# Attention with a bias: q and k land as whole rows, and each head is transposed in its own half of the array's columns

## The chip, the cores and the metric

The kernel runs on one core of one Trainium2 chip. The metric is the device time of one execution in microseconds. Before the change the median of three runs is 240.04 us (239.69 to 240.31).

TensorE (PE) multiplies matrices: a weight load (PEld) puts a tile of 128 rows into the array, a matmul streams the other operand past it and writes to PSUM. ScalarE (ACT) and VectorE (DVE) read PSUM and SBUF, GpSimd (POOL) and SyncE (SP) issue the DMAs here.

## The reference

```python
batch, n_heads, seq_len, head_dim = 4, 8, 1024, 64      # q, k, v; bias is (1, 1, 1024, 1024)
scores = (1 / sqrt(head_dim)) * q @ k.transpose(0, 1, 3, 2) + bias
scores_max = np.max(scores, axis=-1, keepdims=True)
attn = np.exp(scores - scores_max) / (np.sum(np.exp(scores - scores_max), axis=-1, keepdims=True) + 1e-8)
return attn @ v
```

All inputs are float32 with a spread of 0.1, and the kernel takes no maximum out.

## The kernel before

**Tiles.** The 32 heads form 16 pairs. Queries and keys of a head are cut into 8 chunks of 128 (row p * 8 + c lies in partition p, chunk c). A *slot* is one chunk of 128 queries of one head against all 1024 keys; there are 256. A slot's scores stand transposed, keys in the partitions, in one of three PSUM *places* (`pl`), two banks each.

**Scores.** Both heads of a pair share the 128 partitions: 64 values of the one above 64 of the other. A place takes the bias once (L241) and is then never cleared: for the odd head, `ko` against `qo` adds the new scores and takes those of the head before away, because the upper half of `qo` carries a minus sign. For the even head, `ke` and `qe` do the same across two pairs. `qs` and `qz` start a sequence. `fill` (L246) issues the eight matmuls of a slot.

**Exponentials.** ACT takes exp of a whole place (L258, 128x1024). For 20 of the 256 slots DVE computes it instead, in six steps (L272 to L296). `av` (L303) multiplies the result with V, which has a column of ones for the sum; six or seven slots share a bank of PSUM (`po`). `evac` (L315) divides, and SP stores.

**q and k.** POOL loads them with a cast to bf16.
- Pairs below EARLY = 7 land as whole rows (`load_k` L136, `load_q` L145), a head after the other: [128, 2 heads, 8 chunks, 64]. DVE then sets the two heads side by side per chunk (`side_by_side` L159, the copy at L163; `arrange` L455 puts it in the queue).
- Later pairs land side by side at once: one DMA for each head, in pieces of 64 values (L140, L149). `later` (L131) takes buffers from two pools, three of `land` and two of `raw`; `frees` (L475) says what must be free first.
- `transposes` (L188) turns a chunk of both heads with one matmul against an identity (L192), 128 columns of weights. DVE copies the result out as `ko` or `qo` (`copy_out` L195). `ke`, `qe` and the rest come from `ko` and `qo`, by DVE or POOL (`double` L203) or by SP's DMAs (`copy` L552). For q of later pairs DVE first writes -qo over the landed tile (`negate` L215), from which SP copies.

**Order.** The order on each engine is written out at build time by a planner: a loop (L797) that always issues what its model says can start first. It holds prices in ns (`FILL` 452 for a slot's scores, `EXP` 906, 56 for each transposed chunk, L668) and due times for pairs (`DUE`). Half a tile's transposes are one step (`begin`, `end`, L671 to L676), placed between fills and products with V. The first pair has its own code (L335 to L392): q and k of pair 0 land as float32 and are cast and set side by side by DVE and ACT.

Of the kernel before, what the change touches and what calls it, by code (L numbers as in the profile page):

```python
# [9 lines left out]
BF = mybir.dt.bfloat16  # L10
ACTF = mybir.ActivationFunctionType
ALU = mybir.AluOpType
# [4 lines left out]
def kernel(  # L17
# [13 lines left out]
    nc = tc.nc  # L31
    B, H, S, D = q.shape
    P = 128
# [15 lines left out]
    RING = 9  # L49
    NE = 13  # L50
# [77 lines left out]

    LANDS = 5

    def later(pr, x):  # L131
        if (pr - EARLY) % LANDS > 2:
            return raw.tile([P, NCH, 2, D], BF, name=x + "r")
        return land.tile([P, NCH, 2, D], BF, name=x + "16")

    def load_k(pr):  # L136
        if pr >= EARLY:
            raws[pr, 1, 0] = t = later(pr, "k")
            for x in range(2):
                nc.gpsimd.dma_start(out=t[:, :, x, :], in_=kf[pr][:, x].rearrange("p (c d) -> p c d", d=D))  # L140
            return
        lands[pr, 1] = t = land.tile([P, 2, NCH, D], BF, name="k16")
        nc.gpsimd.dma_start(out=t.rearrange("p t c d -> p t (c d)"), in_=kf[pr])

    def load_q(pr, cs):  # L145
        if pr >= EARLY:
            raws[pr, 0, 0] = t = later(pr, "q")
            for x in range(2):
                nc.gpsimd.dma_start(out=t[:, :, x, :], in_=qf[pr][:, x].rearrange("p (c d) -> p c d", d=D))  # L149
            return  # L150
# [5 lines left out]
        nc.gpsimd.dma_start(out=to.rearrange("p t c d -> p t (c d)"),  # L156
                            in_=qf[pr][:, :, cs.start * D:cs.stop * D])

    def side_by_side(pr, x, cs):  # L159

        n = cs.stop - cs.start
        raws[pr, x, cs.start] = t = raw.tile([P, NCH, 2, D], BF, name="qk"[x] + "r")
        nc.vector.tensor_copy(t[:, :n].rearrange("p c t d -> p t c d"), lands[pr, x][:] if pr == 0 else lands[pr, x][:, :, cs, :])  # L163
# [24 lines left out]
    def transposes(pr, which, c0, n, tag, px=None, at=0, to=None):  # L188
        if px is None:
            px = ps_x.tile([P, n, P], BF, tag=tag, name="px")  # L190
        for c in range(at, to or n):
            nc.tensor.transpose(px[:, c, :], raws[pr, which, c0][:, c].rearrange("p t d -> p (t d)"), ident[:])  # L192
        return px
# [141 lines left out]
    with tc.manual_schedule():  # L335
# [28 lines left out]
        kr0 = [raw.tile([P, NCH, 2, D], BF, name="kr") for i in range(2)]  # L364
# [6 lines left out]
        nc.vector.tensor_copy(kr0[0][:, :half].rearrange("p c t d -> p t c d"), k0f[:, :, :half])  # L371
        nc.scalar.copy(braw[:, 0, :], b0f[:])
        nc.scalar.copy(kr0[1][:, :half].rearrange("p c t d -> p t c d"), k0f[:, :, half:])
# [26 lines left out]
        land_at = {(1, 1, 0): 10800, (1, 0, 0): 11500, (2, 1, 0): 14300, (2, 0, 0): 16000, (1, 0, C0): 16800}  # L400
# [9 lines left out]
        raw_at = {}  # L410
# [21 lines left out]
        b_tag, closed = [], []  # L432
        LAG, AVG = 7, 247
# [21 lines left out]
        def arrange(pr, which, c0, n):  # L455

            if pr >= EARLY:
                return
            urgent = need_at[pr, which, c0] - next_fill < 12
            cost = 90 + 40 * n  # L460

            def run(t2):
                side_by_side(pr, which, slice(c0, c0 + n))
                raw_at[pr, which, c0] = t2 + cost + L_DVE + SLACK
                if which == 0 and c0 + n == NCH:
                    freed(pr, t2)
            dve_q.append((land_at[pr, which, c0], 0 if urgent else 2, cost, run))
# [7 lines left out]
        def frees(pr):  # L475

            if pr - LANDS >= EARLY:
                return [pr - LANDS]
            return [pr - 3] if pr < EARLY + 3 else ["raw"]
# [25 lines left out]
        def early(kind, pr):  # L505
            if kind == "k":
                load_k(pr)
                land_at[pr, 1, 0] = dma(pool(0, 750), 1350)
            elif kind == "q":
                load_q(pr, slice(0, NCH) if pr >= SPLIT else slice(C0, NCH))  # L510
                land_at[pr, 0, 0 if pr >= SPLIT else C0] = dma(pool(0, 750), 1350 if pr >= SPLIT else 850)
            elif kind == "v":
                load_v(pr)
                vland_at[pr] = dma(pool(0, 750), 1500)
                move_v(pr)
            else:
                nc.gpsimd.dma_start(out=braw[:, pr, :], in_=bf_[:, pr, :])
                bias_at[pr] = dma(pool(0, 650), 1550)
# [72 lines left out]
        def pe_cands():  # L591
# [66 lines left out]
            if pieces:  # L658
# [4 lines left out]
                if ((pr, which, c0) in raw_at and next_fill >= need - AHEAD and (ring < 0 or last_slot[ring] < next_fill)  # L663
# [4 lines left out]
                    cost = (n // 2 if half_done else to) * 56  # L668
                    urgent = need - next_fill < 12
                    if r < 1e11:  # L670
# [5 lines left out]
                        def end(t, pr=pr, which=which, c0=c0, n=n, tag=tag, cost=cost):  # L676
# [3 lines left out]
                            items = k_items if which else q_items  # L680
                            i = items.index((pr, which, c0, n)) + 2
                            if i < len(items):
                                arrange(*items[i])
                            if pr < EARLY and pieces[0][0] == EARLY:
                                freed("raw", t)
# [109 lines left out]
        for x in k_items[:2] + q_items[:2]:  # L795
            arrange(*x)
# [70 lines left out]
```

## Time and profile before

| what | value |
|---|---|
| median of three runs | 240.04 us |
| the profiled execution's own time | 240.75 us |
| its span, first to last instruction | 239.0 us |
| TensorE clock granted, mean | 0.993 |
| HBM read, written | 29.36 MB, 8.39 MB |

A row of the profile's groups names line, engine, operation, what is written <- what is read, shapes and xcount; then busy us and mean ns of one; then the engine's idle time just before them and what ended it. A window row gives the stretch, its length, and for each engine the busy us and (xcount), then the granted clock, the DMA share and GB/s. A wait row gives us in total, times, and the longest. A timeline row gives start, length, engine, line, operation and, in brackets, the idle time before and its releaser; "issue" means that nothing in the profile released it. "Idle before" of ACT by PE means that no filled place was there.

### The profile page before, as it was taken

The numbers are of one execution on the slowest core, as the hardware profiler recorded it, in microseconds if no ns is written. First come the engines' busy times: TensorE is split into PE (matmuls) and PEld (weight loads), VectorE is DVE, ScalarE is ACT, GpSimd is POOL, SyncE is SP. The second block draws the span as 40 slices with busy tenths as digits, with TensorE's granted clock in tenths as the row PEclk, the third lists the DMA queues.
The fourth block names the chain that finished last, engine by engine and source line by source line (L and its number), as shares of the span: only waits on it lengthen the run. The fifth ranks groups of instructions, "written<-read, shape, count | busy, mean of one in ns | idle before, by whom it ended". The sixth has DMA issues, their size and how long they took to land.

```text
span 239.0 us, 10326 instructions
## 1 busy us (share of the span) xinstructions
PE 221.5 (93%) x4498; PEld 210.1 (88%) x4498; DVE 206.5 (86%) x303; ACT 221.5 (93%) x241; POOL 69.4 (29%) x90
## 2 busy tenths in 40 slices
PE   7889978799996999999998999999999999999991
PEld 2889978699996999999997899999999999999881
DVE  2577879999995989989996989999899999999951
ACT  4699988899997899999999899999999999999991
POOL 8846318589775305142920000000000000000000
PEclk9999999999999999999999999999999999999997
DMA  6999999999999999798999641211112102212111
GB/s 212 191 204 214 226 230 223 197 152 168 177 202 175 136 186 100 159 122 175 155 171 184 163 118 41 69 38 28 50 36 65 47 3 63 58 36 74 36 43 49
DMA packets 87901, 29.74 MB, mean 124 GB/s; under 512 B 67824, under 2 KB 84208, under 8 KB 87856
## 3 DMA queue, kind: packets, MB, share of 16 engines
q0 software_dynamic: 62880, 14.06, 65.8%
q1 hardware_dynamic: 24832, 14.50, 24.3%
q8 instruction: 35, 0.57, 1.0%
q10 hardware_dynamic: 144, 0.52, 0.8%
q14 instruction: 10, 0.08, 0.1%
HBM read 29.36 MB, written 8.39 MB: 158 GB/s over the span
## 4 chain that ended last, share of the span: by engine, by line
PE 58%; ACT 15%; DMA 11%; DVE 7%; issue 5%; POOL 2%; SPq 2%; DVEq 0%; ACTq 0%; POOLq 0%
PE pl L244 35%; PE po L312 16%; ACT E L258 15%; DMA v<-in_v_dram 5%; PE px L192 4%; DMA out_dram<-ob 3%; PE pl L241 3%; DMA braw<-in_bias_dram 2%; DVE qe L212 1%; SPq L711 1%; DVE ob L322 1%; DVE dy L275 1%; DVE qo L201 1%; DVE ko L199 1%; DVE qr L163 1%
## 5 line engine op out<-in xcount | busy, mean ns | idle before, releaser
L258 ACT ACTIVATE E<-pl 128x1024 bf16<-128x1024 f32 (+1 forms) x237 | 218.3, 1087 | 8.3 <-PE pl L244 7.9
L312 PE MATMUL po<-vall,E 128*128 128x65 bf16 x1888 | 89.8, 194 | 1.9 <-ACT E L258 1.0
L312 PEld LDWEIGHTS <-E 128*128 128x128 bf16 x1888 | 76.5, 98 | 2.7 <-ACT E L258 1.4
L244 PE MATMUL pl<-qo,ko 128*128 128x128 bf16 x1024 | 76.6, 219 | 1.6 <-issue 0.4
L244 PEld LDWEIGHTS <-ko 128*128 128x128 bf16 x1160 | 70.6, 98 | 7.4 <-issue 3.5
L244 PE MATMUL pl<-qe,ke 128*128 128x128 bf16 x888 | 65.4, 219 | 2.7 <-DVE qe L212 1.5
L244 PEld LDWEIGHTS <-ke 128*128 128x128 bf16 x888 | 53.8, 98 | 5.3 <-issue 1.4
L275 DVE TENSOR_SCALAR dy<-pl 128x1024 int32<-128x1024 f32 x20 | 24.5, 1223 | 6.6 <-PE pl L244 6.3
L322 DVE TENSOR_TENSOR ob<-po,rs 128x384 f32<-128x384 f32 (+3 forms) x41 | 23.5, 574 | 5.1 <-DMA out_dram<-ob 3.2
L287 DVE SCALAR_TENSOR_TENSOR df<-dt,df 128x1024 f32<-128x1024 f32 x20 | 24.4, 1218 | 0.1
L290 DVE SCALAR_TENSOR_TENSOR dt<-df,dt 128x1024 f32<-128x1024 f32 x20 | 24.4, 1218 | 0.0
L284 DVE SCALAR_TENSOR_TENSOR dt<-df 128x1024 f32<-128x1024 f32 x20 | 24.3, 1217 | 0.0
L295 DVE SCALAR_TENSOR_TENSOR de<-dy,dt 128x1024 uint16<-128x1024 int32 x20 | 24.4, 1218 | 0.0
L149 POOL DMA_DIRECT2D q<-in_q_dram x12 | 10.5, 875 | 20.7 <-PE po L312 7.7
L173 POOL DMA_DIRECT2D vall<-in_v_dram x18 | 16.0, 893 | 1.7 <-DMA k<-in_k_dram 0.9
L280 DVE TENSOR_SCALAR df<-dy 128x1024 f32<-128x1024 uint16 x20 | 14.2, 716 | 0.0
L201 DVE TENSOR_SCALAR qo<-px,sgn 128x1024 bf16<-128x1024 bf16 (+2 forms) x18 | 12.4, 687 | 1.5 <-PE px L192 1.3
L320 DVE RECIPROCAL rs<-po 128x6 f32<-128x6 f32 (+3 forms) x41 | 7.9, 194 | 5.3 <-PE po L312 4.8
L140 POOL DMA_DIRECT2D k<-in_k_dram x12 | 11.0, 916 | 4.4 <-PE px L192 3.0
L199 DVE COPY ko<-px 128x1024 bf16<-128x1024 bf16 (+1 forms) x16 | 10.7, 671 | 1.1 <-PE px L192 1.0
L241 PE MATMUL pl<-ident,braw 128*128 128x128 bf16 x136 | 11.5, 228 | 0.1
L241 PEld LDWEIGHTS <-braw 128*128 128x128 bf16 x136 | 9.9, 148 | 0.3 <-DMA braw<-in_bias_dram 0.3
(56 smaller groups left out, 132.6 us busy)
## 6 DMA issues: line engine op xcount, KB each, us to landing
out_dram<-ob SPq DMA_DIRECT2D x52, 64.0 KB, 2.1
out_dram<-ob SPq DMA_DIRECT2D x30, 96.0 KB, 4.2
ke<-ko SPq DMA_DIRECT2D x22, 128.0 KB, 5.3
vall<-in_v_dram POOLq DMA_DIRECT2D x18, 128.0 KB, 7.6
out_dram<-ob SPq DMA_DIRECT2D x62, 32.0 KB, 1.8
braw<-in_bias_dram POOLq DMA_DIRECT2D x7, 256.0 KB, 8.7
v<-in_v_dram POOLq DMA_DIRECT2D x7, 256.0 KB, 8.1
k<-in_k_dram POOLq DMA_DIRECT2D x6, 256.0 KB, 8.7
```

What stands on the lines that cost most here:

```text
L173: nc.gpsimd.dma_start(out=vall[:, (2 * pr + t) % VR, :, :D], in_=vf[pr, :, t])
L201: nc.vector.tensor_scalar(t["qo"][:, cs, :], px[:], sgn[:], None, op0=ALU.mult)
L241: nc.tensor.matmul(to, braw[:, c, :].rearrange("p (kp kc) -> p kc kp", kc=NCH)[:, kc, :], ident8[:], start=i == 0, stop=False, skip_group_ ...
L244: nc.tensor.matmul(to, kk[:, kc, :], qq[:, c, :], start=False, stop=True, skip_group_check=True)
L258: nc.scalar.activation(e[:, i:i + n].rearrange("p b x -> p (b x)"), places[slots[s][0]][:, i:i + n].rearrange("p b x -> p (b x)"), ACTF.Ex ...
L275: w.tensor_scalar(t["y"][:], places[slots[s][0]].rearrange("p b x -> p (b x)"), scale * LOG2E * 65536.0, 127.0 * 65536.0, op0=ALU.mult, op ...
L284: w.scalar_tensor_tensor(t["t"][:], t["f"][:], -G, t["f"][:], op0=ALU.add, op1=ALU.mult)
L287: w.scalar_tensor_tensor(t["f"][:], t["t"][:], Q, t["f"][:], op0=ALU.mult, op1=ALU.add)
L290: w.scalar_tensor_tensor(t["t"][:], t["f"][:], V, t["t"][:], op0=ALU.add, op1=ALU.mult)
L295: w.scalar_tensor_tensor(etile[s].bitcast(U16).rearrange("p c q -> p (c q)"), t["y"][:], 1.0 / 512.0, t["t"][:], op0=ALU.mult, op1=ALU.add)
L312: nc.tensor.matmul(po[:, j + i, :], etile[s][:, kc, :], vall[:, slots[s][2] % VR, kc, :], start=j + i + kc == 0, stop=kc == NCH - 1, skip_ ...
L322: nc.vector.tensor_tensor(ob[:, :n, :], po[:, :n, :D], rs[:, :n, :].to_broadcast([P, n, D]), op=ALU.mult)
```

## The change

q and k of all pairs from 1 on land as whole rows, one DMA for both heads, in five buffers for each of the two; the pool `raw` and the copies that set heads side by side go. The transposes read the landed rows: each chunk takes two matmuls, one for each head, with 64 columns of weights, the first in the array's columns 0 to 63, the second in 64 to 127 (`tile_position`). They write the upper and the lower 64 partitions of the same PSUM tile. Pair 0's first chunks stay as they were, in buffers of another pool (`de`). The planner's prices for the DMAs and for a transposed chunk (60 instead of 56) are changed, and with them the order on all engines.

```diff
+    LANDS = 5
-    land = ctx.enter_context(tc.tile_pool(name="land", bufs=3))
+    land = ctx.enter_context(tc.tile_pool(name="land", bufs=LANDS))
-    raw = ctx.enter_context(tc.tile_pool(name="raw", bufs=2))
...
     def load_k(pr):
-        if pr >= EARLY:
-            raws[pr, 1, 0] = t = later(pr, "k")
-            for x in range(2):
-                nc.gpsimd.dma_start(out=t[:, :, x, :], in_=kf[pr][:, x].rearrange("p (c d) -> p c d", d=D))
-            return
         lands[pr, 1] = t = land.tile([P, 2, NCH, D], BF, name="k16")
         nc.gpsimd.dma_start(out=t.rearrange("p t c d -> p t (c d)"), in_=kf[pr])
...
-    def side_by_side(pr, x, cs):
-
-        n = cs.stop - cs.start
-        raws[pr, x, cs.start] = t = raw.tile([P, NCH, 2, D], BF, name="qk"[x] + "r")
-        nc.vector.tensor_copy(t[:, :n].rearrange("p c t d -> p t c d"), lands[pr, x][:] if pr == 0 else lands[pr, x][:, :, cs, :])
...
         for c in range(at, to or n):
-            nc.tensor.transpose(px[:, c, :], raws[pr, which, c0][:, c].rearrange("p t d -> p (t d)"), ident[:])
+            if (pr, which, c0) in raws:
+                nc.tensor.transpose(px[:, c, :], raws[pr, which, c0][:, c].rearrange("p t d -> p (t d)"), ident[:])
+                continue
+
+            for t in range(2):
+                nc.tensor.transpose(px[t * D:(t + 1) * D, c, :], lands[pr, which][:, t, c + c0 * (pr > 0), :], ident[:],
+                                    tile_position=(0, t * D))
...
-        t = raws[pr, 0, 0].rearrange("p c t d -> p c (t d)")
-        nc.vector.tensor_scalar(t[:], arrs[pr]["qo"][:], -1.0, 1.0, op0=ALU.mult, op1=ALU.mult)
+        t = lands[pr, 0].rearrange("p t c d -> p (t c d)").rearrange("p (c x) -> p c x", x=P)
+        nc.vector.tensor_scalar(t, arrs[pr]["qo"][:], -1.0, 1.0, op0=ALU.mult, op1=ALU.mult)
...
+        TR = 60
...
-            while loads and all(x in free_lands for x in frees(loads[0])):
+            while loads and loads[0] - LANDS in free_lands:
                 load(loads.pop(0), t)
...
-                land_at[pr, x, 0] = raw_at[pr, x, 0] = dma(pool(pool(t, 900), 900), 2350)
+                raw_at[pr, x, 0] = dma(pool(t, 900), 1600) + SLACK
...
-                v_at[p] = dma(pool(t, 1900), 2400)
+                v_at[p] = dma(pool(t, 1900), 4300)
...
-                    cost = (n // 2 if half_done else to) * 56
+                    cost = (n // 2 if half_done else to) * TR
```

More of the change, by code (lines that the diff above doesn't have):

```diff
@@ L126 @@
     raws, lands, arrs = {}, {}, {}
[L129 to L134, printed above, removed]
-    def load_k(pr):
-        if pr >= EARLY:
-            raws[pr, 1, 0] = t = later(pr, "k")
-            for x in range(2):
-                nc.gpsimd.dma_start(out=t[:, :, x, :], in_=kf[pr][:, x].rearrange("p (c d) -> p c d", d=D))
-            return
+    def load_k(pr):
         lands[pr, 1] = t = land.tile([P, 2, NCH, D], BF, name="k16")
@@ L145, in load_q @@
     def load_q(pr, cs):
[L146 to L150, printed above, removed]
         if pr == 0:
@@ L363 @@
         qr0 = raws[0, 0, 0] = consts.tile([P, C0, 2, D], BF, name="qr0")
-        kr0 = [raw.tile([P, NCH, 2, D], BF, name="kr") for i in range(2)]
+        kr0 = [de.tile([P, NCH, P], BF, name="de")[:, :half].rearrange("p c (t d) -> p c t d", d=D) for i in range(2)]
         raws[0, 1, 0], raws[0, 1, half] = kr0
@@ L370 @@
         nc.vector.tensor_copy(qr0.rearrange("p c t d -> p t c d"), q0f[:])
-        nc.vector.tensor_copy(kr0[0][:, :half].rearrange("p c t d -> p t c d"), k0f[:, :, :half])
+        nc.vector.tensor_copy(kr0[0].rearrange("p c t d -> p t c d"), k0f[:, :, :half])
         nc.scalar.copy(braw[:, 0, :], b0f[:])
-        nc.scalar.copy(kr0[1][:, :half].rearrange("p c t d -> p t c d"), k0f[:, :, half:])
+        nc.scalar.copy(kr0[1].rearrange("p c t d -> p t c d"), k0f[:, :, half:])
         pq = transposes(0, 0, 0, C0, "xa")
@@ L453, in keys @@
             return [("ke", pr), ("ke1", pr), ("qe", pr, part(pr, c)), ("qe1", pr, part(pr - 1, c))]
[L455 to L467, printed above, removed]
         def freed(pr, t):
             free_lands.add(pr)
-            while loads and all(x in free_lands for x in frees(loads[0])):
+            while loads and loads[0] - LANDS in free_lands:
                 load(loads.pop(0), t)
[L475 to L479, printed above, removed]
         def load(pr, t):
@@ L679, in end @@
                             half_done.clear()
[L680 to L685, printed above, removed]
+                            if pr < EARLY and which == 0 and c0 + n == NCH:
+                                freed(pr, t)
                             def run(t2):
@@ L794 @@
             early(x[0], int(x[1]))
-        for x in k_items[:2] + q_items[:2]:
-            arrange(*x)
         while next_fill < NS or next_act < len(acts) or avq or dav or dve_q or sp_q:
```

11 lines of the change are left out of this document (5 added, 6 removed).

## The prediction

> **What bounds the kernel now.** I read the page's busy times first, then the waits of ScalarE (ACT) and a table of three stretches: 12 to 48 us (the head, loads still arriving), 48 to 138 us (the middle) and 138 to 234 us (the rest).
>
> ```profile
> PE 221.5 (93%) x4498; PEld 210.1 (88%) x4498; DVE 206.5 (86%) x303; ACT 221.5 (93%) x241; POOL 69.4 (29%) x90
> PE 58%; ACT 15%; DMA 11%; DVE 7%; issue 5%; POOL 2%; SPq 2%; DVEq 0%; ACTq 0%; POOLq 0%
> ...
> 12.00:48.00 36.00, 31.03 (x623) 29.35 (x621) 30.34 (x63) 33.08 (x36) 18.31 (x25) 1.00 1.30 215
> 48.00:138.00 90.00, 86.11 (x1815) 84.16 (x1813) 81.87 (x111) 86.17 (x94) 41.01 (x46) 1.00 1.59 162
> 138.00:234.00 96.00, 93.72 (x1971) 89.78 (x1968) 88.47 (x112) 95.87 (x105) 0.00 (x0) 1.00 0.19 49
> ...
> ACT E L258 <- PE pl L244: 2.6, 5, 1.0
> ACT E L258 <- PE pl L244: 3.8, 6, 1.6
> ```
>
> The columns of the table are PE, PEld, DVE, ACT, POOL; the two last rows are ACT's waits in the head and in the middle. ACT is the floor: 95.87 of 96 us at the end, 86.17 of 90 us in the middle. What can be won is what it waits, all of it for fills of PE: 2.6 us and 3.8 us, 6.4 in all. The granted clock is 1.00 throughout.
>
> Whether PE has room is not read from its busy time, since its matmuls overlap. So I price them by their spacing, (length of a run less one matmul) over (count less one), and multiply by the counts of the lines.
>
> ```profile
> L312 PE MATMUL po<-vall,E 128*128 128x65 bf16 x1888 | 89.8, 194 | 1.9 <-ACT E L258 1.0
> L244 PE MATMUL pl<-qo,ko 128*128 128x128 bf16 x1024 | 76.6, 219 | 1.6 <-issue 0.4
> L241 PE MATMUL pl<-ident,braw 128*128 128x128 bf16 x136 | 11.5, 228 | 0.1
> ...
> 25.42 1.50 PE L244 MATMUL pl<-qe,ke 128*128 128x128 bf16 x24
> 26.76 0.68 PE L312 MATMUL po<-vall,E 128*128 128x65 bf16 x16
> 27.72 0.61 PE L192 MATMUL px<-ident,kr 128*128 128x128 bf16 x8
> 48.62 0.66 PE L241 MATMUL pl<-ident,braw 128*128 128x128 bf16 x8
> ```
>
> A score takes (1.50 - 0.219)/23 = 0.0557 us, a matmul with V (0.68 - 0.194)/15 = 0.0324, a transpose (with the score's 0.219) (0.61 - 0.219)/7 = 0.0559, a bias matmul (0.66 - 0.228)/7 = 0.0617.
>
> ```profile
> 12.00:48.00 36.00, 19.99 (x286) 16.87 (x287) 1.00 1.30 215
> 48.00:138.00 90.00, 60.55 (x822) 49.15 (x819) 1.00 1.59 162
> 12.00:48.00 36.00, 10.38 (x240) 9.08 (x240) 1.00 1.30 215
> 48.00:138.00 90.00, 37.44 (x800) 32.20 (x800) 1.00 1.59 162
> 12.00:48.00 36.00, 7.68 (x97) 5.70 (x94) 1.00 1.30 215
> 48.00:138.00 90.00, 10.21 (x137) 8.23 (x138) 1.00 1.59 162
> 48.00:138.00 90.00, 4.75 (x56) 4.07 (x56) 1.00 1.59 162
> ```
>
> These are L244, L312 and L192 in head and middle, and L241 in the middle. The middle needs 822 x 0.0557 + 800 x 0.0324 + 137 x 0.0559 + 56 x 0.0617 = 45.8 + 25.9 + 7.7 + 3.5 = 82.9 us of 90; the head 15.9 + 7.8 + 5.4 = 29.1 us of 36. So in the middle PE has 7.1 us free, in the head 6.9. It is nearly a second floor, and that is where this change adds work.
>
> **Stops that the change could remove.** Two of the middle's holes are of one kind.
>
> ```profile
> 73.78 0.33 PE L244 MATMUL pl<-qz,ko 128*128 128x128 bf16 x3
> 76.09 0.44 PE L244 MATMUL pl<-qz,ko 128*128 128x128 bf16 x5 [1.97 <-issue]
> ...
> 129.78 0.22 PE L244 MATMUL pl<-qo,ko 128*128 128x128 bf16 x1
> 130.39 0.55 PE L244 MATMUL pl<-qo,ko 128*128 128x128 bf16 x7 [0.38 <-issue]
> 131.02 0.62 DVE L322 TENSOR_TENSOR ob<-po,rs 128x448 f32<-128x448 f32 x1 [1.72 <-DMA out_dram<-ob]
> ...
> 74.05:130.35 56.30, 53.76 (x1144) 52.56 (x1142) 49.79 (x67) 54.08 (x60) 21.30 (x24) 1.00 1.42 156
> ...
> q0 software_dynamic: 62880, 14.06, 65.8%
> q8 instruction: 35, 0.57, 1.0%
> q0 software_dynamic: 8823, 6.21, 113.8%
> ...
> 76.62 1.02 ACT L258 ACTIVATE E<-pl 128x1024 bf16<-128x1024 f32 x1 [1.59 <-PE pl L244]
> 78.28 1.02 ACT L258 ACTIVATE E<-pl 128x1024 bf16<-128x1024 f32 x1 [0.63 <-PE pl L244]
> 132.94 1.99 ACT L258 ACTIVATE E<-pl 128x1024 bf16<-128x1024 f32 x2 [0.48 <-PE pl L244]
> 135.58 1.94 ACT L258 ACTIVATE E<-pl 128x1024 bf16<-128x1024 f32 x2 [0.65 <-PE pl L244]
> ```
>
> PE stops inside a run of eight matmuls, released by nothing. Queue q8 carries 35 packets for 2 x 4498 PE instructions, 257 each; between the stops stand 1144 + 1142 = 2286, which is 8.9 packets. I read both stops as instructions that arrived late behind a full DMA. ACT loses 1.59 + 0.63 and 0.48 + 0.65 us there, 3.35 of its 3.8; at 131 us a store that lands late (1.72) takes part.
>
> **The change, part by part.** (1) Fourteen copies at L163 go from DVE.
>
> ```profile
> 10.00:46.00 36.00, 5.88 (x14) 1.00 1.24 215
> POOL q L156 <- DVE qr L163: 3.9, 2, 3.3
> ```
>
> That is 5.88 us, all in the head, and with five landing buffers POOL no longer waits 3.9 us for those copies. ACT waits only 2.6 us there, which bounds the gain; nothing moves the loads themselves, which fill the DMA engines (215 GB/s).
>
> (2) From pair 7 on, k and q land in whole rows: 9 pairs x 4 head-tensors x 128 x 8 = 36,864 of q0's 62,880 packets become 4,608 longer ones. A q0 packet took 0.658 x 16 x 239 / 62880 = 0.040 us; in the head, where long ones rule, 1.138 x 16 x 36 / 8823 = 0.074. So 36864 x 0.040 / 16 = 92 us of all engines shrink to about 21. Stores, V and instructions should land sooner: worth between 0 and the 3.35 us above; I take all of it where PE leaves room. POOL issues 18 loads instead of 36, hidden, as it is busy 29%; V loads and whatever follow in its queue are not delayed by fewer issues.
>
> (3) A chunk is transposed by two matmuls into 64 columns each instead of one into 128: 245 chunks (11 at the start stay whole), 490 matmuls where 245 were. In the order of the changed program they stand in 43 stretches, so PE goes into the half-width form and back 86 times: 28 before slot 40 (96 chunks), 50 in slots 40 to 143 (133 chunks, the middle), 8 after. No row shows this form. Per chunk the cost is between 0.056 (halves side by side) and 0.112 us (one after the other). Per change of form it is between 0, as L244, L312 and L192 now follow each other, and 0.219 - 0.056 = 0.163, the part of a matmul that the next one usually covers. With nothing nearer to either end I take the middle of both, 0.084 and 0.08.
>
> The row for a change of form is only that bound. The Trainium skill, page "TensorEngine Tiling (Array Packing)", Key Properties, says that "Changing tiling mode (not just tile) drains the TensorE", and under Restrictions that column tiling disables Fast Weight Load; both speak against the change and no run here shows them. By the Trainium skill's page "TensorE: Matmul & The Clock Gate", LDWEIGHTS, 64 columns would load in 64/1.2 = 53 ns, so about 0.107 us a chunk (an estimate), which is the serial end.
>
> Middle: 133 x (0.084 - 0.056) + 50 x 0.08 = 3.7 + 4.0 = 7.7, so 90.6 us of PE work. PE has not been seen full: without its stops it did 82.9 in 90 - 2.4 = 87.6 (95%). I take 97%, between that and 100: 90.6 / 0.97 = 93.4, 3.4 longer than 90, the removed stops included. Head: 96 x 0.028 + 28 x 0.08 = 4.9, covered by PE's 6.9 us free and set off by the copies: 0 (bounds -2.6 and +3.1, the latter from 96 x 0.056 + 28 x 0.163 - 6.9). Rest: 16 x 0.028 + 8 x 0.08 = 1.1, behind ACT: 0. Sum: 240.75 + 3.4 = 244.1 against the profiled execution's time (239.0 span); the runs' median, 240.04, is 0.7 lower, so **243.4**.
>
> **Rivals.** *Halves overlap and the form changes cheaply:* at 0.060 a chunk and 0.03 a change the middle needs 82.9 + 0.5 + 1.5 = 84.9, / 0.97 = 87.5, below 90: 2.5 won, and some 0.6 of the head's waits, 236.9. For it: all full-width kinds run at their spacing now, and ACT's stops in the middle really coincide with PE's. Against: it needs two prices near their low ends at once. It decides as soon as the extra work in the middle is under 82.9 + 4.4 = 87.3, that is 4.4 us. The Trainium skill, page "TensorE: Matmul & The Clock Gate", Measured speedup vs the span model, gives three column tiles 2.38 times the speed of one; by that the chunk would lie at this end.
>
> *Halves one after the other:* 0.112 with 0.08 gives 82.9 + 7.4 + 4.0 = 94.3, / 0.97 = 97.2 (+7.2), head + 0.7: 248. With 0.163, 98.5 / 0.97 = 101.5 (+11.5), head +3.1: 254.6. For it: each half has its own weight load. Against: weight loads of 128 columns keep a spacing of 0.032 now.
>
> *Nothing comes of it:* the copies were off ACT's path and the stops are repaid by PE: within 0.3%.
>
> **Numbers.** Forecast 0.40, with its own range 240.8 to 246.5; overlap 0.37; serial 0.15; nothing 0.08. A measurement of this kernel tells 0.3% from no change, 0.7 us. Faster 0.37, same 0.08, slower 0.55. The range 235.5 to 249.5 leaves out the serial case with dear changes and the last of the overlap case.
>
> **What will show it.** In the changed profile: the spacing of the half-width matmuls (0.028 against 0.056 each), and the gap from the last of them to the next score; L163 gone; q0 near 30,000 packets and no stop by issue of over 1 us; PE at 6.00 of 6 us in the middle with ACT waiting for L244. If ACT is unbroken from 60 to 138 us, I am wrong and the first rival holds; stops by issue that stay would refute step 2.

## The result: faster by 0.6%, and the profile after

The changed kernel takes 238.5 us, the median of four runs (238.25 to 238.87), against 240.04 us before: a ratio of 0.9938, with a 95% interval of 0.9919 to 0.9957. The forecast was 243.4, slower. The time lies inside the wide range (235.5 to 249.5), below the forecast's own range (240.8 to 246.5), and on the other side of no change. Here and below, medians are of all executions, while the ratios leave out the slow ones, those over 1.5% above the fastest of the same kernel. The profiled execution took 238.87 us with a span of 236.8 us (before 240.75 and 239.0), so the two profiles differ by 2.2 us of span.

The page after: busy time, the chain of work that ended last, two DMA queues, and the half-width transposes of q as a group.

```profile
PE 227.0 (96%) x4743; PEld 211.0 (89%) x4743; DVE 197.8 (84%) x287; ACT 222.9 (94%) x241; POOL 50.1 (21%) x72
PE 69%; ACT 16%; issue 7%; DMA 4%; POOL 3%; ACTq 1%; DVE 0%; POOLq 0%
...
q0 software_dynamic: 30336, 14.06, 47.2%
q8 instruction: 37, 0.61, 1.1%
...
L173 PE MATMUL px<-ident,q 128*64 128x128 bf16 x240 | 11.0, 223 | 0.1
```

PE is busier and has 245 matmuls more, as counted in the forecast. DVE no longer stands in the chain (7% before), and q0's packets are halved. L173 is now the half-width transpose. Next come the three stretches of the forecast with the same columns (PE, PEld, DVE, ACT, POOL), and what ACT waits for PE in the head and in the middle.

```profile
12.00:48.00 36.00, 34.42 (x738) 31.14 (x736) 24.42 (x54) 34.00 (x37) 16.59 (x24) 1.00 1.19 214
48.00:138.00 90.00, 88.88 (x1927) 83.73 (x1925) 81.21 (x109) 87.75 (x94) 23.44 (x29) 1.00 1.09 160
138.00:234.00 96.00, 93.37 (x1983) 89.47 (x1980) 87.35 (x111) 94.53 (x103) 0.00 (x0) 1.00 0.20 52
...
ACT E L240 <- PE pl L226: 1.8, 5, 0.8
ACT E L240 <- PE pl L226: 1.5, 5, 0.5
```

ACT, the floor, is busier in the middle (87.75 us against 86.17) and waits less there (1.5 us against 3.8). A stretch of fixed bounds mixes the work of different slots, so I followed slots instead. This table gives the start of the first score matmul of a slot, in us from the span's start, read from the trace:

```
slot              16      40      72     128     144     255   span
before         22.27   47.70   76.62  123.56  138.88  231.29  239.0
after          22.46   46.03   74.48  122.92  137.76  230.32  236.8
lead of after  -0.19    1.67    2.14    0.64    1.12    0.97    2.2
```

Up to slot 40 the changed kernel wins 1.67 us. From slot 40 to 144 it needs 91.73 us where before needed 91.18, 0.55 longer. At the last slot 0.97 us are left. The other 1.23 us come after it.

Single profiles scatter, though. before_tail (below) has before's order on PE to the last matmul, and its slot 40 starts at 46.91 us, its last slot at 230.12; after_again is the changed kernel once more, and its slot 40 starts at 46.73. So leads of under about 1 us in this table may be chance. What repeats is the direction in the head: four traces with the changed kernel's order on PE have slot 40 at 46.03 to 46.73, two with before's order at 46.91 and 47.70. From slot 40 to 144 the same traces take 90.97 to 91.73 and 90.80 to 91.18 us, which is no clear difference.

Two timelines show the end, first after, then the same place before.

```profile
233.07 0.43 PE L294 MATMUL po<-vall,E 128*128 128x65 bf16 x8 [0.48 <-ACT E L240]
233.54 0.17 DVE L302 RECIPROCAL rs<-po 128x1 f32<-128x1 f32 x1 [0.28 <-PE po L294]
233.75 0.23 DVE L304 TENSOR_TENSOR ob<-po,rs 128x64 f32<-128x64 f32 x1
```

```profile
234.04 0.43 PE L312 MATMUL po<-vall,E 128*128 128x65 bf16 x8 [0.48 <-ACT E L258]
234.51 0.17 DVE L320 RECIPROCAL rs<-po 128x1 f32<-128x1 f32 x1 [0.42 <-PE po L312]
236.20 0.23 DVE L322 TENSOR_TENSOR ob<-po,rs 128x64 f32<-128x64 f32 x1 [1.52 <-DMA out_dram<-ob]
```

Before, the last output tile waited 1.52 us for a store that still read its buffer. The pool `op` has two. The planner cut the last slots into banks of 6, 2 and 1; after the change they are 6, 4 and 1, and the store is done in time. The diff touches nothing there. It is a first sign that the order changed, and not the edit.

What the half-width form costs can be read from one stretch of the timeline.

```profile
86.86 0.61 PE L226 MATMUL pl<-qo,ko 128*128 128x128 bf16 x8
87.39 0.64 PE L173 MATMUL px<-ident,k 128*64 128x128 bf16 x16
87.97 0.62 PE L226 MATMUL pl<-qe,ke 128*128 128x128 bf16 x8
```

The spacing by the forecast's own formula is (0.64 - 0.223) / 15 = 0.028 us for a half, so 0.056 for a chunk, as much as one full-width transpose. In the raw starts the two halves of a chunk are 3 to 4 ns apart and chunks 56: the halves run side by side. The change of form does cost. Eight scores and eight chunks at 0.056 from 86.86 on would let the next scores start at 87.76; they start at 87.97, 0.21 later. By medians of the raw starts, going into the form adds 0.093 us, coming out 0.096, and the first chunk takes 0.024 longer, together 0.213 for a stretch.

The Trainium skill, page "TensorEngine Tiling (Array Packing)", Key Properties, says that changing the tiling mode drains TensorE; the trace agrees that a change costs time, 0.09 us each, and does not show whether TensorE drains. The Restrictions of the same page of the Trainium skill say that column tiling loses Fast Weight Load, and from the Trainium skill's page "TensorE: Matmul & The Clock Gate", LDWEIGHTS, I had estimated 0.107 us a chunk; the trace shows 0.056, and the measurement decides.

### The profile page after: what moved, and what is told of

Read it like the earlier page. It is cut to its first block, busy times and chain, and to the rows that moved or that the text cites. A ratio compares the mean times of both kernels' runs of the same rounds, so it can differ in the third digit from the quotient of the medians.

```text
span 236.8 us, 10752 instructions
## 1 busy us (share of the span) xinstructions
PE 227.0 (96%) x4743; PEld 211.0 (89%) x4743; DVE 197.8 (84%) x287; ACT 222.9 (94%) x241; POOL 50.1 (21%) x72
## 3 DMA queue, kind: packets, MB, share of 16 engines
q0 software_dynamic: 30336, 14.06, 47.2%
## 4 chain that ended last, share of the span: by engine, by line
PE 69%; ACT 16%; issue 7%; DMA 4%; POOL 3%; ACTq 1%; DVE 0%; POOLq 0%
PE pl L226 39%; PE po L294 20%; ACT E L240 16%; PE px L173 7%; DMA q<-in_q_dram 4%; PE pl L223 2%; ACTq L817 1%; POOL k L130 1%; POOL braw L336 0%; POOL qz L332 0%; POOL qs L333 0%; POOL q L138 0%; POOL v L145 0%; POOL ident masks.py:199 0%; DVE ob L304 0%
## 5 line engine op out<-in xcount | busy, mean ns | idle before, releaser
L294 PE MATMUL po<-vall,E 128*128 128x65 bf16 x1888 | 92.3, 194 | 1.9 <-ACT E L240 1.0
L294 PEld LDWEIGHTS <-E 128*128 128x128 bf16 x1888 | 77.6, 98 | 2.8 <-ACT E L240 1.4
L226 PEld LDWEIGHTS <-ko 128*128 128x128 bf16 x1160 | 69.0, 98 | 5.3 <-issue 1.0
L226 PE MATMUL pl<-qe,ke 128*128 128x128 bf16 x888 | 66.3, 219 | 1.6 <-DVE qe L194 0.6
L226 PEld LDWEIGHTS <-ke 128*128 128x128 bf16 x888 | 52.6, 98 | 5.1 <-issue 1.0
L304 DVE TENSOR_TENSOR ob<-po,rs 128x448 f32<-128x448 f32 (+3 forms) x40 | 23.4, 585 | 1.5
L138 POOL DMA_DIRECT2D q<-in_q_dram x16 | 11.5, 719 | 42.9 <-PE pl L226 33.0
L302 DVE RECIPROCAL rs<-po 128x7 f32<-128x7 f32 (+3 forms) x40 | 7.9, 197 | 11.8 <-PE po L294 11.4
L173 PE MATMUL px<-ident,q 128*64 128x128 bf16 x240 | 11.0, 223 | 0.1
```

The lines of the kernel that those rows point to most:

```text
L173: nc.tensor.transpose(px[t * D:(t + 1) * D, c, :], lands[pr, which][:, t, c + c0 * (pr > 0), :], ident[:], tile_position=(0, t * D))
L226: nc.tensor.matmul(to, kk[:, kc, :], qq[:, c, :], start=False, stop=True, skip_group_check=True)
L294: nc.tensor.matmul(po[:, j + i, :], etile[s][:, kc, :], vall[:, slots[s][2] % VR, kc, :], start=j + i + kc == 0, stop=kc == NCH - 1, skip_ ...
L304: nc.vector.tensor_tensor(ob[:, :n, :], po[:, :n, :D], rs[:, :n, :].to_broadcast([P, n, D]), op=ALU.mult)
```

## Experiments

Medians in us, and the ratio to the kernel before with its 95% interval. In these batches the kernel before had a median of 240.6 to 241.0.

### The form alone, and the end alone

before_half keeps the order of before and its copies, and transposes pairs 1 to 15 and pair 0's later chunks as two half-width matmuls.

```diff
-            nc.tensor.transpose(px[:, c, :], raws[pr, which, c0][:, c].rearrange("p t d -> p (t d)"), ident[:])
+            for t in range(2):
+                nc.tensor.transpose(px[t * D:(t + 1) * D, c, :], raws[pr, which, c0][:, c, t, :], ident[:],
+                                    tile_position=(0, t * D))
```

> The kernel before, in its own order on every engine, with only the transposes of pairs 1 to 15 and of pair 0's later chunks made in two half-width matmuls each. Theory (a change of form costs PE 0.094 us, the pair of halves no more than one full matmul, and PE is nearly a second floor): 66 changes, 6.2 us more PE work, some of it in PE's free time: 1 to 4 us longer than before, 241 to 244 us. Rival (a change of form is covered by the matmuls around it, as the shown gap of 0.15 us is only latency): 240.0, within 0.7 us.

Measured: 243.81, ratio 1.0126 (1.0062 to 1.0191), 2.9 us more than before by the medians and 3.0 by the ratio, with the last slot's fill 1.23 us later in the profile. The form costs time when nothing is given back for it. Its profile also keeps the stops; two are over 1 us:

```profile
76.11 0.20 PE L317 MATMUL po<-vall,E 128*128 128x65 bf16 x1 [1.32 <-issue]
128.53 0.55 PE L249 MATMUL pl<-qe,ke 128*128 128x128 bf16 x7 [1.43 <-issue]
```

before_tail gives the last, one-slot output tile of before a buffer of its own.

```diff
+    oblast = consts.tile([P, 1, D], F32, name="oblast")
-        ob = op.tile([P, 7, D], F32, name="ob")
+        ob = op.tile([P, 7, D], F32, name="ob") if n > 1 else oblast
```

> The kernel before, with a buffer of its own for the last, one-slot output tile. Theory (1.2 us of the change's gain is at the very end, where before the last division waited 1.5 us for a store that still read its buffer): 1.2 to 1.5 us shorter than before, about 238.7 us. Rival (the end is set by the landing of the last stores, whichever tile they read): no change, 240.0 us.

Measured: 239.94, 0.9966 (0.9927 to 1.0004). In the profile, from the end of the last product with V to the end of the span it takes 3.4 us instead of 4.5, which is near the theory's size. Over the runs it can't be told from no change.

### The copies and the landing

after_copies puts the copies by DVE back into the changed kernel, into a buffer that nobody reads. They are 14 (DVE's count goes from 287 to 301), not the 15 that the expectation names.

```diff
+        if at == 0 and pr < EARLY and (pr, which, c0) not in raws:
+            src = lands[pr, which][:] if pr == 0 else lands[pr, which][:, :, c0:c0 + n, :]
+            dst = dp.tile([P, S], F32, name="dt").bitcast(BF)[:, :n * P].rearrange("p (c t d) -> p t c d", t=2, d=D)
+            nc.vector.tensor_copy(dst, src)
```

> The changed kernel with 15 copies of landed q and k tiles put back on DVE (into a buffer nobody reads), each just ahead of the tile's transposes, so only DVE's load in the first 46 us is as before. Theory (the head's gain of about 1 us came from DVE): 0.7 to 1.3 us longer than the changed kernel, about 239.5 us. Rival (it came from the landing buffers and the loads): 238.5 us, within 0.4.

Measured: 238.41, 0.9898 (0.9862 to 0.9934), slot 40 at 46.16. DVE's load was not where the head's gain came from, and (1) of the forecast, at 0, was right.

after_pieces lets k and q of pairs 7 to 15 land in pieces of 64 values again, four DMAs for a pair, without touching the order of the work. The rows have a gap of two values in SBUF, and a buffer of zeros is moved for the room.

```diff
+        flat = land.tile([P, 2 * NCH * (D + 2)], BF, name=x + "16")
+        if pr >= EARLY:
+            return flat.rearrange("p (t c d) -> p t c d", t=2, c=NCH)[:, :, :, :D], flat
...
+            for x in range(2):
+                nc.gpsimd.dma_start(out=t[:, x], in_=kf[pr][:, x].rearrange("p (c d) -> p c d", d=D))
```

> The changed kernel with k and q of pairs 7 to 15 loaded in pieces of 64 values again, one DMA for each head (rows with a gap of two values after each piece); the order on every other engine is the changed kernel's. Theory (whole rows shortened PE's stops for late instructions): the stops grow from at most 0.66 us to 1 us or more at least once, and the time by 0.5 to 2 us, 239 to 240.5 us. Rival (PE is full in the middle, so the stops only moved): 238.5 us, within 0.4.

Measured: 240.28, 0.9973 (0.9942 to 1.0003). That is 1.9 us over after_copies, which ran beside it with the same order on PE, and 1.8 over the changed kernel itself in another batch (after_again below). Its one profile is of an execution of 243.11 us, far from its median, so its times are not compared. Its stops are these:

```profile
61.45 0.29 PE L311 MATMUL po<-vall,E 128*128 128x65 bf16 x4 [0.71 <-issue]
68.65 1.33 PE L243 MATMUL pl<-qe,ke 128*128 128x128 bf16 x21 [0.79 <-issue]
77.31 0.47 PE L240 MATMUL pl<-ident,braw 128*128 128x128 bf16 x5 [2.11 <-issue]
```

In the changed kernel, at the same places of the same order, PE stopped by 0.2 us:

```profile
67.42 1.33 PE L226 MATMUL pl<-qe,ke 128*128 128x128 bf16 x21 [0.16 <-issue]
74.16 0.48 PE L223 MATMUL pl<-ident,braw 128*128 128x128 bf16 x5 [0.20 <-issue]
```

This is as (2) had it: small packets go with longer stops, and with a longer time. That the 1.8 us lie in just these stops is not shown, for want of a profile near the median.

after_lands3 leaves three landing buffers instead of five.

```diff
-    LANDS = 5
+    LANDS = 3
```

> The changed kernel with three landing buffers instead of five; the order on PE, DVE and ACT is the same until pair 7 and beyond, only POOL's loads of pairs 4 to 6 have to wait for transposes. Theory (the head's 1.3 us came from loads that no longer wait for a buffer): slot 40 starts 0.7 to 1.6 us later than in the changed kernel, the time 239 to 240 us. Rival (it came from the order and the shorter way from landing to transposes): slot 40 within 0.3 us, 238.5 us.

Measured: 240.64, 1.0008 (0.9968 to 1.0049), slot 40 at 45.72. The number of buffers isn't the head's gain; what this kernel loses, it loses after slot 144 (started at 136.77, 0.99 ahead of the changed kernel), beside a stop of 1.2 us that ends at 138.72.

### The order of the halves and the number of stretches

after_again is the changed kernel once more, for the batches.

> The changed kernel once more, as the measure for the runs beside it: 0.9938 of the kernel before, 238 to 239 us.

Measured: 238.44, 0.9924 (0.9887 to 0.9960).

after_serial issues all of a step's chunks of one head ahead of the other head's. A step is half a tile, so four matmuls of one head stand ahead of four of the other.

```diff
-                continue
-
-            for t in range(2):
+        for t in range(0 if (pr, which, c0) in raws else 2):
+            for c in range(at, to or n):
```

> The changed kernel with all chunks of the first head transposed ahead of those of the second within a step, instead of in turn. Theory (two half-width matmuls overlap only where they stand in different columns, so a chunk costs 0.056 us in turn and 0.112 one after the other): 7.4 us more PE work in the middle and 5.4 in the head, 244 to 250 us. Rival (a half's weight load overlaps either way and the matmuls run at the same rate): 238.5 us, within 1.

Measured: 238.5, 0.9915 (0.9877 to 0.9953). The timeline has the same stretch of 16 in 0.66 us instead of 0.64:

```profile
62.45 0.66 PE L172 MATMUL px<-ident,k 128*64 128x128 bf16 x16
```

So the halves need not alternate to overlap. In the raw starts the first matmul of the second head begins 13 ns after the first of the first head (62.453 and 62.466 us), though four stand ahead of it: the two column halves work off their matmuls as two streams, over four instructions at least. The theory's 244 to 250 us fell.

after_whole puts both halves of a tile's transposes into one stretch: 60 changes of form instead of 86.

```diff
+            if half_done:
+                return next(x for x in c if x[2].__name__ == "end")
```

> The changed kernel with the two halves of a tile's transposes always in one stretch, so 60 changes of form instead of 86, 32 instead of 50 in the middle. Theory (each stretch costs PE 0.093 + 0.096 + 0.024 us beyond its chunks, and PE is the bound of the middle): 1.9 us less PE work there, the time 0.4 to 1.5 us shorter than the changed kernel. Rival (a longer stretch keeps fills back, ACT waits for them): the same or up to 1 us longer.

Measured: 240.22, 0.9958 (0.9910 to 1.0005). Up to slot 112 it leads the changed kernel, at 107.89 against 108.46. Then one stop gives it back:

```profile
121.61 0.52 PE L294 MATMUL po<-vall,E 128*128 128x65 bf16 x11 [1.76 <-issue]
```

This kernel has q0's 30,336 packets too. Whole rows don't rule such a stop out, and the run doesn't settle what fewer changes are worth.

### What gave the head's 1.7 us: the way of the rows, or the planner's prices

after_sbs lets DVE set pairs 1 to 6 side by side again and transposes them full width, in the order of the changed kernel on ACT, POOL and SP; later pairs stay half-width. That takes 28 changes of form away.

```diff
+        raws[pr, x, cs.start] = t
+        nc.vector.tensor_copy(t.rearrange("p c t d -> p t c d"), lands[pr, x][:] if pr == 0 else lands[pr, x][:, :, cs, :])
...
+            dve_q.append((raw_at[pr, which, c0] - SLACK, -1, 0, run))
```

> The changed kernel with pairs 1 to 6 set side by side by DVE again, read from there by full-width transposes, two buffers each for q and k as before; ACT, POOL and SP keep the changed kernel's order, DVE's differs by the 15 copies alone, PE's not at all but for the form of the early transposes (28 changes of form fewer). Theory (the head's gain is the shorter way from landing to transposes): slot 40 starts at 47 us or later, as before the change, and the time is 0.7 to 1.6 us longer than the changed kernel's. Rival (the gain is the changed planner prices and the order that they give): slot 40 at 45.5 to 46.7 us, as in the changed kernel, 238 to 238.8 us.

Measured: 238.13, 0.9870 (0.9822 to 0.9918), slot 40 at 45.21, earlier than with the change. So the way without DVE is hardly the gain. The run doesn't isolate it: the 28 changes of form that went with it are 14 x 0.213 = 3.0 us of PE's work, which could hide a loss.

after_price tells the planner what the form costs, 56 for a chunk and 213 for a stretch.

```diff
-                    cost = (n // 2 if half_done else to) * TR
+                    cost = (n // 2 if half_done else to) * 56 + 213
```

> The changed kernel with the measured price in the planner: 56 ns a chunk plus 213 ns for each stretch, instead of 60 a chunk; the order on the engines follows. Theory (PE is the bound of the middle, so an order that knows the price wastes less): up to 1 us shorter than the changed kernel, 237.4 to 238.4 us. Rival (PE's work is what counts, not where the planner thinks it stands): 238.5 us, within 0.5, or longer if the new order stops more often for late instructions.

Measured: 243.85, 1.0102 (1.0053 to 1.0151). A truer price made another order, 5.4 us worse than the changed kernel's. The rival allowed a longer time by stops for late instructions, but the trace has one such stop, of 1.1 us. It shows more of the loss elsewhere: the new order cuts the transposes into 56 stretches instead of 43 (13 x 0.213 = 2.8 us more of PE's time) and gives DVE 22 exponentials instead of 20. ACT waits for PE 9.3 + 2.4 us (the first two rows) instead of 4.9 in the changed kernel (the third):

```profile
ACT E L240 <- PE pl L226: 9.3, 15, 2.1
ACT E L240 <- PE po L294: 2.4, 5, 0.6
...
ACT E L240 <- PE pl L226: 4.9, 13, 0.8
```

That left the order itself as the suspect. The next two runs cross it with the change. before_prices is the kernel before with the new prices of DMAs:

```diff
-                v_at[p] = dma(pool(t, 1900), 2400)
+                v_at[p] = dma(pool(t, 1900), 4300)
-                land_at[pr, 1, 0] = dma(pool(0, 750), 1350)
+                land_at[pr, 1, 0] = dma(pool(0, 750), 1600)
-                land_at[pr, 0, 0 if pr >= SPLIT else C0] = dma(pool(0, 750), 1350 if pr >= SPLIT else 850)
+                land_at[pr, 0, 0 if pr >= SPLIT else C0] = dma(pool(0, 750), 1600 if pr >= SPLIT else 1100)
-                vland_at[pr] = dma(pool(0, 750), 1500)
+                vland_at[pr] = dma(pool(0, 750), 1600)
-                bias_at[pr] = dma(pool(0, 650), 1550)
+                bias_at[pr] = dma(pool(0, 650), 1600)
```

> The kernel before with nothing but the changed kernel's prices for DMAs in its planner (1600 for 1350, 1100 for 850, V 1600 for 1500 and 4300 for 2400, bias 1600 for 1550), so the same work in another order. Theory (the head's 1.7 us come from the order that these prices make): slot 40 starts near 46.0 us instead of 47.7, time 238.0 to 239.5. Rival (they come from the landing of whole rows itself, the loads or the copies): slot 40 at 47.4 to 48.0, time as before, ratio 0.998 to 1.002. Should the time be worse by over 1 us, the order is a lottery that neither theory forecasts.

after_prices_back is the changed kernel with all these lines, and TR, as before (56 for 60). The price of the later pairs' loads, which the change took from 2350 for two DMAs to 1600 for one, is not set back.

> The changed kernel with the prices of before (DMAs, and 56 for a transposed chunk instead of 60), so the change without the new prices. Theory (the head's gain is the prices' order): slot 40 starts near 47.5 us instead of 46.0, and the time is about 240. Rival (the gain is the change's own): slot 40 at 46.0 within 0.3 and a time of 238.0 to 239.0. In both, stops by issue stay below 0.7 us, since whole rows stay.

Measured:

```
                        old prices                       new prices
work of before          240.0 (241.0 in this batch)      235.78  ratio 0.9798 (0.9759 to 0.9838)
work of the change      240.78  1.0004 (0.9965-1.0042)   238.5   ratio 0.9938 (0.9919 to 0.9957)
```

The prices alone, five numbers that are in no instruction, win 2% on the old work. On the new work they win 0.7% by the ratios. The change at its old prices wins nothing. Slot 40 starts at 45.99 in before_prices, as the theory had it.

In after_prices_back the time is the theory's, but the place is not. Slot 40 starts at 46.59, within the 46.03 to 46.73 of the changed order's own traces, so setting the prices back did not take the head's lead away. Beside the changed kernel it is 0.79 us late at slot 144, 0.72 at the last slot and 1.62 at the end of the span: its last output tiles hold 6, 6 and 1 slots instead of 6, 4 and 1. Its stops by issue reach 0.83 us, where both theories kept them below 0.7.

Nor is the work of before_prices quite the same: the planner also decides which slots DVE computes, 19 instead of 20, and its last tiles hold 6, 4 and 1 slots instead of 6, 2 and 1. Here are the stretches of before_prices, and ACT's waits for PE in head and middle:

```profile
12.00:48.00 36.00, 32.18 (x643) 30.68 (x641) 29.44 (x68) 33.68 (x37) 19.21 (x26) 1.00 1.31 215
48.00:138.00 90.00, 88.36 (x1868) 86.41 (x1867) 83.44 (x111) 88.87 (x97) 40.73 (x46) 1.00 1.59 163
...
ACT E L258 <- PE pl L244: 2.1, 3, 0.9
ACT E L258 <- PE pl L244: 1.3, 2, 1.0
...
q0 software_dynamic: 62880, 14.06, 66.7%
```

ACT is busy for 88.87 of 90 us in the middle, more than in either kernel, with the old 62,880 packets. Its longest stop by late instructions is this one:

```profile
73.61 0.34 PE L312 MATMUL po<-vall,E 128*128 128x65 bf16 x5 [0.59 <-issue]
```

So a stop over 1 us does not need to appear with the packets there, either.

### What the form costs in the better order

before_prices_half adds the edit of before_half to before_prices; the order stays.

> The kernel of before_prices (235.78) with the transposes of pairs 1 to 15 and of pair 0's later chunks as two half-width matmuls each, the order untouched: nothing but the form is added. Theory (0.094 us for each change of form and 0.024 for the first chunk of a stretch, in a PE that is nearly full until slot 144): some 50 changes between slots 40 and 144 are 5 us of PE work, of which ACT's free time covers part, so 237.0 to 239.0, slot 144 at 135.5 to 137.5 instead of 134.31. Rival (the form is hidden by PE's idle time, and the change loses to before_prices by its order alone): 235.4 to 236.4 and slot 144 within 0.5 of 134.31.

Measured: 241.36, 1.0017 (0.9980 to 1.0054), so 5.6 us above before_prices, more than the theory's 1.2 to 3.2. The order holds 35 stretches, and 35 x 0.213 = 7.5 us of PE's time. Its start of slot 40 is 1.93 us later than in before_prices, that of slot 128 3.59, that of slot 144 5.75, and the last fill 5.55. In the last jump lies a stop that before_prices didn't have:

```profile
129.24 0.40 PE L317 MATMUL po<-vall,E 128*128 128x65 bf16 x7 [1.48 <-issue]
130.12 2.96 ACT L263 ACTIVATE E<-pl 128x1024 bf16<-128x1024 f32 x3 [0.98 <-PE pl L249]
```

The stop and the 0.98 us that ACT loses behind it were not in the theory's sum; the remaining 4 us are near the 5 us that it had before deducting ACT's cover.

### Is the better order a matter of right prices?

Five more orders of the same kind come from raising all the early DMAs' prices by one step.

```diff
-                land_at[pr, 1, 0] = dma(pool(0, 750), 1350)
+                land_at[pr, 1, 0] = dma(pool(0, 750), 1400)
```

This is the step of before_plus50, with 900, 1550 and 1600 for the other three. The others go up by 100, 400 and 700 in the same lines, and after_plus200 raises those of the changed kernel by 200.

> The kernel before with each of the four prices of early DMAs raised by 50 (1400, 900, 1550, 1600): another order of the same work. Theory (the order is a draw: any small change of a price gives another one, good or bad, with a spread of some us): 236 to 243, with no reason to fall between 240.0 and 235.8. Rival (higher prices are nearer the truth, and the gain comes by degrees): between 239 and 240.5.

> The same with each price raised by 100 (1450, 950, 1600, 1650). Theory (a draw): 236 to 243, and not between the time of before_plus50 and 235.8 other than by chance. Rival (by degrees): 237.5 to 239.5, below before_plus50.

> The kernel before with the prices of its early DMAs raised by 400 (1750, 1250, 1900, 1950). By degrees (a load that is priced too low makes the planner put its readers where they wait): at or below 236.5, or up to 1 us worse once the price is above the truth. A draw: anywhere from 236 to 243.

> The same raised by 700 (2050, 1550, 2200, 2250). By degrees: within 1.5 us of before_plus400. A draw: anywhere from 236 to 243.

> The changed kernel with the same prices raised by 200 (1800, 1300, 1800, 1800). By degrees: 237.0 to 238.5, at or below the changed kernel's 238.5. A draw: 236.5 to 243.

Measured, with the runs above:

```
work of before     +0 241   +50 239.17   +100 238.0   new prices 235.78   +400 239.58   +700 243.16
work of the change          old prices 240.78         new prices 238.5    +200 242.39   form priced 243.85
```

The first four of before's work fall one after the other, and the last two rise again (the new prices are not quite on this line: they raise the loads of q and k by 250, those of V by 100 and the bias by 50, and later V by 1900). By degrees had it right for +50 and +100 and wrong for the three others: +400 was to stay at or below 237.5, +700 within 1.5 us of that, and the changed kernel's +200 at or below 238.5, where it took 3.9 us more. A best price near +250 for before's work isn't excluded by these points, nor is chance. A draw did no better: +100 came out between +50 and 235.8, which it allowed only by chance, and +700 just above its 243. So six orders of the old work span 7.4 us (235.78 to 243.16), and four of the changed kernel's 5.4 us. Both spans are wider than the difference that was to be forecast. Which order is good, none of my theories says.

## Why the forecast was wrong

**The bound** was right: PE stands at 88.88 of 90 us in the middle, ACT waits only for PE, and what is won or lost is what ACT waits. "If ACT is unbroken from 60 to 138 us, I am wrong" is nearly what came: it is busy for 75.90 of those 78 us, where before it was 74.21.

**(1), the copies**: taken at 0, and 0 by after_copies.

**(2), the stops**: in the changed kernel no stop by issue between slots 40 and 144 is longer than 0.66 us in the raw starts, and the long ones come back when rows land in pieces (after_pieces). Four traces of the changed kernel's order on PE have none over 0.66, and three of before's (before, before_tail, before_half) each have one of 1.6 us or more. So the step holds for this pair. As a rule it is too simple: before_prices has the small packets and no stop over 0.8 us, and after_whole has whole rows and one of 1.95 us.

That the stops are late instructions can be settled from the packets in the traces. All 41 stops by issue of 0.3 us and more, in 20 traces, stand at the same instruction of each 256 of PE, number 193 or 194 from 0 with weight loads, matmuls and PE's own waits counted. Each ends 1.2 to 1.7 us after a packet of q8, 16,384 bytes, has ended, and nowhere does PE get past that place sooner than 1.2 us after its packet. The packet itself takes only 0.9 to 1.5 us there: it starts late. In the kernel before, from 145 us on, when the loads are over, each packet starts between 0.1 us before and 1.3 us after PE passes number 193 of the 256 ahead (median 0.0). From 48 to 138 us the median is 2.4, and the packets of the two stops, at 5.2 and 3.9, are the two latest. In after_pieces the three stops' packets start 4.3, 4.8 and 6.0 us after it, those of the changed kernel at the same places 3.6, 4.1 and 4.1. This fits a packet that waits behind the loads, as the forecast read the stops; what else could delay its start, no run separates. The order moves both the loads and PE, and no run tells beforehand which order avoids a stop. The Trainium skill, page "Runtime: NRT & Kernel Launch", section Instruction fetch mechanics, has such refills in blocks of 16 KiB (256 instructions); q8's packets agree in size.

**(3), the transposes**: here sits the mis-sized term. I took a chunk at 0.084 us, the middle of my bounds; it is 0.056, the low end, and 3.7 us of the middle's 7.7 go. The change of form at 0.08 was close: 0.094, and 0.024 for the first chunk. With the measured prices the middle's extra work is 50 x 0.094 + 25 x 0.024 = 5.3 us, and 82.9 + 5.3 = 88.2, / 0.97 = 90.9: 0.9 longer than 90 instead of 3.4. Measured from slot 40 to slot 144 it was 0.55 longer, with traces of one order up to 0.8 apart. The middle's sum, then, fits once the chunk is priced rightly. As the order had changed as well, part of the fit may be luck, and the 97% to which PE could be filled was a guess that no run tests by itself. With the chunk alone put right the forecast would still have been about 240.9, no gain. (The head's upper bound, given as 3.1, comes to 3.0 from its own terms; nothing hangs on it.)

**The term that was not in the sum** decided the sign. The forecast counted its stretches in the changed program's order, but took the waits, the stops and the head and end from before's, and so put the change of the order, which the diff made by prices, at nothing. It is worth -2.3 us on the changed work (240.78 to 238.5; -1.6 by the ratios, since the batches differ) and -5.2 on the old (241.0 to 235.8). Of the span's 2.2 us, in the two profiles, 1.67 came by slot 40 and 1.23 from the last store's buffer, and 0.7 were given back between. The second is the order's: no edit touches that place. The first was not found in the copies or the number of buffers; since it stays with the old prices (46.59), what gave it in the changed kernel is open.

**The edit by itself**, in an order left alone, is only measured in parts: the form costs 2.9 us in before's order and 5.6 in the better one; the landing in whole rows gave 1.8 in the changed kernel's order (by the ratios 1.2 against after_again, with intervals that overlap, and 1.8 against after_copies of the same batch, with intervals that don't). As one whole it was 0 at the old prices and +2.7 us at the new ones (3.4 by the ratios), each with an order of its own. So the edit was slower at the new prices, as forecast, and without effect at the old; it was the kernel with its order that became faster. Two rivals lie about equally near the time: "nothing" at 240.0 and the first at 236.9, 1.5 and 1.6 us off. Neither has the mechanism: the stops were not simply repaid by PE, and in the first the halves do overlap, but the form changes dearly.

## What to carry to other kernels

Where a planner writes the order, treat the order as a term of its own: cross the new prices with the old work before crediting the edit, since here five prices won 2% on the old work and the edit, at its old prices, nothing. The best kernel of this study is before_prices, 235.78 us, 2.0% below before and about 1% below the change; and it, too, is one of ten orders of the two kernels, which spread over 8 us. One kernel's own executions spread over several us too (before's from 238.6 to 244.4 in all batches), so an order is judged by several runs. A half-width matmul pair costs what one full-width matmul does if its halves lie in different columns; pay attention instead to how often PE goes into that form and out again, 0.2 us each time around. By that price longer stretches should cost less, but the one run that made them longer (after_whole) was not faster.

## What the runs showed of the hardware that was not expected

Two matmuls in different column halves overlap whichever way they are issued: alternating, 418 ns from the first to the last start of 16; one head's four ahead of the other's, 445. PE's stops by late instructions, 0.3 to 2.1 us of idle time, all fell on the same place of every 256 instructions, number 193 or 194, in kernels with 30,336 and with 62,880 packets alike, and ended 1.2 to 1.7 us after the packet that brings instructions had ended. Two groups of the changed kernel, weight loads:

```profile
L294 PEld LDWEIGHTS <-E 128*128 128x128 bf16 x1888 | 77.6, 98 | 2.8 <-ACT E L240 1.4 <-issue 1.1
L173 PEld LDWEIGHTS <-q 128*64 128x64 bf16 x240 | 7.4, 109 | 1.9 <-DMA q<-in_q_dram 0.3
```

Those of 64 columns show 109 ns each where those of 128 show 98, and yet nothing of it appears in the spacing of the chunks.
